# A gate's loads and heads' results in rings of tiles, attention steps counted by time, in a hybrid attention and retention layer

## The chip, the core and the metric

The kernel runs on one core of a Trainium2 chip. The metric is the device time of one execution, in microseconds. The core has a matrix engine (TensorE, PE in the rows; the load of its weights is PEld), VectorE (DVE), ScalarE (ACT), GpSimd (POOL) and SyncE (SP), which here issues most DMAs. Each engine takes its instructions in a fixed order. A chip-wide memory (DRAM) holds inputs, weights and spilled partial results; SBUF holds the tiles, PSUM the banks in which matmuls add up.

## The reference

One layer over 256 latent tokens and 256 context tokens of width 4096: a modulated RMS norm, one input projection of 14336 columns, differential attention in eight heads A (two softmax maps a head) and two-way retention in eight heads B, a SiLU gate on each, one output projection, and a residual with a gate. Cut to what matters:

```python
mod = silu(c) @ ada_w + ada_b
shift, scale, gate = split(mod, 3)
h = rms_norm(x, norm_w) * (1 + scale) + shift          # hc likewise from ctx, c_ctx
proj = h @ w_in                                        # dq dk dv dg rq rk rv rg
pc = hc @ w_ctx                                        # c_dk c_dv c_rk c_rv
o_d = diff_attention(dq, k_all, v_all, lam)            # 8 heads A, 256 wide
o_d = rms_norm(o_d, subln_w) * (1 - lam_init) * silu(dg)
o_r = rms_norm(retention(rq, rk, rv), ret_norm_w) * silu(rg)   # 8 heads B
y = concatenate([o_d, o_r]) @ w_out
return x + gate * y
```

## The kernel before

All products are float32 made of three passes: weights and activations are split into a high and a low part (whi, wlo and h), and each block of 128 rows of depth is hi x hi, hi x lo, lo x hi (L405 to L407). The depth of 4096 is 32 blocks, "kt". A **unit** is two kt of one head's columns: its weights are loaded by SP into a raw tile (three buffers, L387), ScalarE casts them to whi (L392), VectorE subtracts for wlo (L393), three buffers each, and PE multiplies them with 4 row tiles (K and V of latent and context tokens) or 2 (Q and gate of latent tokens). So a head has K/V units on four PSUM banks and Q/G units on two; the pool `mm` has six banks. A head of A is 512 columns wide, of B 384.

The normed input h arrives late, because its modulation needs a product with ada_w. So the work is staged. First, K/V of all A heads for the first ten kt while the modulation is made; then `first_parts`: for each head as many kt as are there, with partial sums copied to a kvqg tile and stored to DRAM (`store_part`, L523, ACT's queue), while VectorE makes the rest of the modulation (L322). Then `rests`: for A0 to A7 and B0 to B7 the remaining units, 104 of A (16, 16, 14, 12, 12, 12, 12, 10) and 140 of B (four heads with 19, four with 16). Four units before the end of a half the partial sums are loaded back (`load_part`, L518, SP's queue) into a kvqg tile, and after the last unit VectorE adds the banks to it (L500), which frees the banks. Last, the output projection, L1061, whose products are called psO.

In `rests`, three things run beside the products. *Attention*: when a head's units are over, `attend` puts its generator (`attA` or `attB`) into the list `tasks`; `bg_step` takes one step of the first in the list. attA has 16 steps, attB 12. Heads are taken strictly one after the other; a step touches PE, ScalarE, VectorE and GpSimd in turn. attA begins with norms (L748), ends its use of K and V with the split of V's second half (L723) and of Q/G with the output's transposes. `to_B` drains the list, closes the pool of attA's tiles and opens attB's. *The gate*: `gate_task` multiplies the last third of ada_w with c on VectorE, 128 loads of 512 KB (L938) and 128 steps (L952); at the end of each quarter the sum is split into gah and gal, which take a buffer each of the tags whi and wlo, until PE has summed them (pg, L963). *Weight loads* of the next unit.

The function `between`, called after each unit, takes one attention step, two when more than one head waits, and gate steps at 132 over the number of units less 8.

The pool `a4` has 39 slots (SLOTS) of 4 KB a partition: h takes one for each kt (22 once the first ten kt are used up), and kvqg tiles, gate loads, their sums and the B heads' outputs take theirs as they come free. What runs in which order on an engine is settled when the program is built, by a scheduler that takes the order of the program as priority; a load is issued when a slot is free for it.

Of the kernel before, what the change touches and what calls it, by code (L numbers as in the profile page):

```python
# [10 lines left out]
F32 = mybir.dt.float32  # L11
# [7 lines left out]
P = 128  # L19
D = 4096  # L20
KT = D // P
# [22 lines left out]
T_COL = 0.457e-3  # L44
# [33 lines left out]
def hybrid_kernel(es, tc, x, c, ctx, c_ctx, norm_w, ada_w, ada_b, w_in, q_norm_w, k_norm_w,  # L78
# [12 lines left out]
    a4 = es.enter_context(tc.tile_pool(name="a4", bufs=SLOTS, side="right"))  # L91
# [13 lines left out]
    def aux_tile(shape, name):  # L105
        return aux.tile(shape, F32, name=name, tag="aux")
# [243 lines left out]
    for half in range(2):  # L350
        ss = adap.tile([P, 2, NX], F32, name=f"ss{half}", tag="ss")
        for i in range(NX):
# [4 lines left out]
            for q in range(2):  # L357
                g = 2 * i + q
# [81 lines left out]
    def run_units(units):  # L440

        it = iter(units)
        nxt = next(it, None)
        if nxt is not None:
            nxt[0].prepare()
        while nxt is not None:
            (u, post), nxt = nxt, next(it, None)
            if nxt is not None:
                nxt[0].prepare()
            u.run()  # L450
            post()
# [13 lines left out]
    def evict(dst, src):  # L465
        evict_flip[0] ^= 1
        if evict_flip[0]:
            nc.scalar.copy(dst, src)
        else:
            nc.vector.tensor_copy(dst, src)  # L470

    class Head:

        def __init__(self, kind, h):
# [5 lines left out]
        def dst(self, rt, qg):  # L480
            i = 2 if qg else rt // 2
            if self.t[i] is None:
                self.t[i] = a4.tile([P, 2, self.ncol], F32, name=f"kvqg{self.name}_{i}", tag="a4")
            return self.t[i][:, rt % 2, :]

    def head_units(hd, qg, ktseq, part=False, rest=False, tag=""):
# [39 lines left out]
    def pairs(a, b):  # L526
        r = []
        while a < b:
            n = min(2, b - a)
            r.append((a, n))  # L530
            a += n
        return r
# [83 lines left out]
    kdone = {(nm, qg): K1 if nm[0] == "A" and not qg else 0 for nm in heads for qg in range(2)}  # L616

    def first_parts():

        items = [(f"B{h}", 0) for h in range(HB)] + [(f"A{h}", 1) for h in range(HA)] + [(f"B{h}", 1) for h in range(HB)]  # L620
        for nm, qg in items + [(f"A{h}", 0) for h in range(HA)]:
            hd = heads[nm]
            a, b = kdone[nm, qg], ada2.avail
            if a < b and not (a > 0 and ada2.done):
                kdone[nm, qg] = b
                nrt = 2 if qg else 4
                spare = FILL * 2 * 3 * nrt * hd.ncol * T_COL - (0.2 + 2 * hd.ncol * 1.05e-3)
                for u in head_units(hd, qg, pairs(a, b), part=True, rest=a > 0, tag=f"p{a}"):
                    yield u, lambda spare=spare: ada2.spend(spare)

    run_units(first_parts())
    while not ada2.done:
        ada2.spend(1.0)
# [86 lines left out]
    def split(hi, lo, src):  # L720

        nc.scalar.copy(hi, src)  # L722
        nc.vector.tensor_tensor(lo, src, hi.bitcast(F32), op=ALU.subtract)  # L723
# [207 lines left out]
    GW = 1024  # L931
    GATE_STEPS = D // GW * (KT + 1)

    def gate_task():
        def load(v):
            cb, kt = divmod(v, KT)
            raw = a4.tile([P, GW], F32, name=f"graw{cb}_{kt}", tag="a4")
            nc.sync.dma_start(raw, ada_w[kt * P:(kt + 1) * P, 2 * D + cb * GW:2 * D + (cb + 1) * GW])  # L938
            return raw

        n = D // GW * KT
        ahead = [load(0), load(1)]
        for v in range(n):
            cb, kt = divmod(v, KT)
            raw = ahead.pop(0)
            if v + 2 < n:
                ahead.append(load(v + 2))
            if kt == 0:
                acc = a4.tile([P, GW], F32, name=f"gacc{cb}", tag="a4")
                nc.vector.tensor_scalar(acc, raw, cT[:, 0, kt:kt + 1], None, op0=ALU.mult)  # L950
            else:
                nc.vector.scalar_tensor_tensor(acc, raw, cT[:, 0, kt:kt + 1], acc, op0=ALU.mult, op1=ALU.add)  # L952
            yield
            if kt == KT - 1:
                ah = wpool.tile([P, GW], F32R, name=f"gah{cb}", tag="whi", bufs=3)
                al = wpool.tile([P, GW], F32R, name=f"gal{cb}", tag="wlo", bufs=3)
                split(ah, al, acc)
                gb = a4.tile([P, GW], F32, name=f"gb{cb}", tag="a4")
                nc.scalar.dma_start(gb[0:1], ada_b[0:1, 2 * D + cb * GW:2 * D + (cb + 1) * GW])
                for q in range(GW // 512):  # L960
                    pg = aux_tile([P, 512], f"pg{cb}_{q}")
                    for i, a in enumerate((ah, al)):
                        nc.tensor.matmul(pg[0:32], onesr, a[:, q * 512:(q + 1) * 512], start=i == 0, stop=i == 1)  # L963
                    nc.vector.tensor_tensor(gb[0:1, q * 512:(q + 1) * 512], pg[0:1, :], gb[0:1, q * 512:(q + 1) * 512], op=ALU.add)
                nc.scalar.dma_start(g_dram[0:1, cb * GW:(cb + 1) * GW], gb[0:1])
                yield


    tasks = []

    def bg_step():
        while tasks:
            try:
                next(tasks[0])
                return
            except StopIteration:
                tasks.pop(0)

    def bg_drain():
        while tasks:  # L980
            bg_step()

    gate = gate_task()
    atB = [None]

    gate_due = [0.0, sum(len(pairs(a, KT)) for a in kdone.values()) - 8]

    def between():
        bg_step()
        if len(tasks) > 1:  # L990
            bg_step()
        gate_due[0] += GATE_STEPS / gate_due[1]
        while gate_due[0] >= 1:
            gate_due[0] -= 1
            next(gate, None)

    def to_B():
        between()
        bg_drain()
        atA_cm.__exit__(None, None, None)  # L1000
        atB_cm = tc.tile_pool(name="attB", bufs=1, side="left")
        atB[:] = [atB_cm.__enter__(), atB_cm]

    def rests():
        for nm in [f"A{h}" for h in range(HA)] + [f"B{h}" for h in range(HB)]:
            hd = heads[nm]
            us = []
            for qg in range(2):
                a = kdone[nm, qg]
                if a < KT:  # L1010
                    us.append(head_units(hd, qg, pairs(a, KT), rest=a > 0))
                else:
                    load_part(hd, qg)

            def attend(hd=hd):
                tasks.append(attA(hd) if hd.kind == "A" else attB(hd, atB[0]))
                between()

            flat = [(u, between) for q in us for u in q]
            if nm == "B0":  # L1020
                k = min(4, len(flat) - 2)
                flat[k] = (flat[k][0], to_B)
            flat[-1] = (flat[-1][0], attend)
            yield from flat

    run_units(rests())
    while next(gate, 0) is None:
# [33 lines left out]
    for nb in range(NB):  # L1061
        bank = Bank(f"psO{nb}", 2)
        start, end = out_ends(nb, bank)
        for i, s in enumerate(order):
            xs = (lambda k, r, s=s: o_t[s][:, 0, k, r * P:(r + 1) * P],
                  lambda k, r, s=s: o_t[s][:, 1, k, r * P:(r + 1) * P])
# [42 lines left out]
```

## Time and profile before

| | us |
|---|---|
| median of three executions | 2659.67 (2658.77 to 2660.13) |
| the profiled execution | 2661.34 |
| its span, first to last instruction | 2659.6 |
| PE busy | 2515.6 |
| VectorE busy | 1820.5 |
| ScalarE busy | 887.6 |
| mean granted clock of PE | 0.969 of full |

Busy times are unions of an engine's instructions over the span. The ends of matmuls are modelled, so a busy PE is not a PE at its peak. Times in rows are in microseconds from the span's start. A wait is put down to the instruction that came last by the semaphores. Products of an A head in `rests` write psA, of a B head psB.

### The profile page before, as it was taken

How to read it: one execution, taken by the hardware profiler on the slowest of the kernel's cores; microseconds unless marked ns; L12 is line 12 of the kernel's file. 1: busy time of each engine (PE TensorE's matmuls, PEld its weight loads, DVE VectorE, ACT ScalarE, POOL GpSimd, SP SyncE). 2: the span in 40 equal slices, each digit the busy share in tenths (PEclk: the TensorE clock that was granted, in tenths of full speed). 3: DMA queues.
4: the chain of work that ended last, by engine and by line, in shares of the span. 5: the costliest groups of instructions: out<-in, count | busy, mean ns of one | idle time of the engine just before them, and what ended most of it. 6: DMA issues, size and time to landing. Idle time of an engine off the chain costs nothing. (4 is left out here: it accounts for less than half of the span.)

```text
span 2659.6 us, 33974 instructions
## 1 busy us (share of the span) xinstructions
PE 2515.6 (95%) x12354; PEld 2140.1 (80%) x12354; DVE 1820.5 (68%) x2438; ACT 887.6 (33%) x1384; POOL 42.7 (2%) x47
## 2 busy tenths in 40 slices
PE   7999999999998999997899999997488999999999
PEld 4677799987988888876688788997388999778887
DVE  4756939799589489797866777564577666644444
ACT  4211222343443122222333344433233333433333
POOL 0000000000000000000000000000000000000000
PEclk8999999999999999997899999999699999999999
DMA  9977858889789678677866566442256564666765
GB/s 319 293 249 223 283 180 269 265 277 328 236 256 314 230 266 258 222 239 260 308 207 191 186 210 190 152 142 74 99 164 226 194 196 153 218 196 209 223 211 171
DMA packets 471417, 590.82 MB, mean 222 GB/s; under 512 B 32521, under 2 KB 353353, under 8 KB 471249
## 3 DMA queue, kind: packets, MB, share of 16 engines
q1 hardware_dynamic: 453392, 544.40, 64.0%
q10 hardware_dynamic: 17856, 44.25, 4.6%
q8 instruction: 97, 1.59, 0.3%
q14 instruction: 72, 0.58, 0.1%
HBM read 551.81 MB, written 36.72 MB: 221 GB/s over the span
## 5 line engine op out<-in xcount | busy, mean ns | idle before, releaser
L322 DVE SCALAR_TENSOR_TENSOR acc<-ada,cT,acc 128x1024 f32<-128x1024 f32 (+1 forms) x372 | 427.9, 1190 | 0.0
L406 PE MATMUL psB<-wloB,h 128*128 128x384 f32 x896 | 305.2, 341 | 2.4 <-DVE wloB L393 2.4
L407 PE MATMUL psB<-whiB,h 128*128 128x384 f32 x896 | 303.3, 339 | 0.0
L405 PE MATMUL psB<-whiB,h 128*128 128x384 f32 x896 | 285.1, 340 | 5.7 <-DVE kvqgB L500 5.7
L393 DVE TENSOR_TENSOR wloO<-rawO,whiO 128x1024 fp32r<-128x1024 f32 x128 | 156.8, 1225 | 173.8 <-ACT whiO L392 173.6
L406 PE MATMUL psA<-wloA,h 128*128 128x512 f32 x560 | 229.4, 410 | 12.0 <-DVE wloA L393 11.9
L405 PE MATMUL psA<-whiA,h 128*128 128x512 f32 x560 | 212.8, 405 | 17.6 <-ACT whiA L392 17.6
L407 PE MATMUL psA<-whiA,h 128*128 128x512 f32 x560 | 226.0, 406 | 0.0
L392 ACT CAST whiO<-rawO 128x1024 fp32r<-128x1024 f32 x128 | 134.5, 1052 | 214.8 <-PE psO L407 172.3
L406 PE MATMUL psO<-wloO,o 128*128 128x512 f32 x512 | 204.1, 399 | 0.3 <-DVE wloO L393 0.3
L407 PE MATMUL psO<-whiO,o 128*128 128x512 f32 x512 | 203.4, 398 | 0.0
L393 DVE TENSOR_TENSOR wloB<-rawB,whiB 128x768 fp32r<-128x768 f32 x140 | 133.2, 955 | 85.0 <-ACT whiB L392 84.4
L392 ACT CAST whiB<-rawB 128x768 fp32r<-128x768 f32 x140 | 116.2, 834 | 216.1 <-PE psB L407 138.5
L405 PE MATMUL psO<-whiO,o 128*128 128x512 f32 x512 | 184.3, 399 | 1.2 <-ACT o L722 1.2
L952 DVE SCALAR_TENSOR_TENSOR gacc<-graw,cT,gacc 128x1024 f32<-128x1024 f32 x124 | 158.8, 1281 | 38.7 <-DMA graw<-in_ada_w_dram 37.6
L392 ACT CAST whiA<-rawA 128x1024 fp32r<-128x1024 f32 x104 | 109.0, 1050 | 201.4 <-PE psA L407 135.4
L405 PEld LDWEIGHTS psB<-whiB,h 128*128 128x128 f32 x896 | 167.7, 190 | 7.5 <-DVE kvqgB L500 6.1
L406 PEld LDWEIGHTS psB<-wloB,h 128*128 128x128 f32 x896 | 169.3, 189 | 4.9 <-DVE wloB L393 4.0
L407 PEld LDWEIGHTS psB<-whiB,h 128*128 128x128 f32 x896 | 169.4, 189 | 0.5
L393 DVE TENSOR_TENSOR wloA<-rawA,whiA 128x1024 fp32r<-128x1024 f32 x104 | 126.5, 1221 | 49.3 <-ACT whiA L392 48.7
L405 PEld LDWEIGHTS psA<-whiA,h 128*128 128x128 f32 x560 | 106.7, 193 | 45.3 <-ACT whiA L392 20.9
L406 PEld LDWEIGHTS psA<-wloA,h 128*128 128x128 f32 x560 | 108.7, 194 | 42.1 <-DVE wloA L393 17.0
(495 smaller groups left out, 5178.9 us busy)
## 6 DMA issues: line engine op xcount, KB each, us to landing
ada<-in_ada_w_dram SPq DMA_DIRECT2D x512, 256.0 KB, 4.6
graw<-in_ada_w_dram SPq DMA_DIRECT2D x128, 512.0 KB, 7.4
rawO<-in_w_out_dram SPq DMA_DIRECT2D x128, 512.0 KB, 4.6
rawA<-in_w_in_dram SPq DMA_DIRECT2D x208, 256.0 KB, 3.7
rawB<-in_w_in_dram SPq DMA_DIRECT2D x140, 256.0 KB, 3.0
p_dramA<-kvqgA ACTq DMA_DIRECT2D x40, 512.0 KB, 4.3
kvqgA<-p_dramA SPq DMA_DIRECT2D x40, 512.0 KB, 6.3
rawB<-in_w_in_dram SPq DMA_DIRECT2D x140, 128.0 KB, 2.4
```

What stands on the lines that cost most here:

```text
L322: nc.vector.scalar_tensor_tensor(acc[v], w, cv, acc[v], op0=ALU.mult, op1=ALU.add)
L392: nc.scalar.copy(hi, raw)
L393: nc.vector.tensor_tensor(lo, raw, hi.bitcast(F32), op=ALU.subtract)
L405: nc.tensor.matmul(pt[:, :ncol], a, hi, start=f, stop=False)
L406: nc.tensor.matmul(pt[:, :ncol], a, lo, start=False, stop=False)
L407: nc.tensor.matmul(pt[:, :ncol], b, hi, start=False, stop=e)
L952: nc.vector.scalar_tensor_tensor(acc, raw, cT[:, 0, kt:kt + 1], acc, op0=ALU.mult, op1=ALU.add)
```

## The change

Before the first parts a ring of four tiles of a4 is made, before the rests one of nine; `Head.dst` takes the next tile of the ring instead of a new slot, so a head's three tiles are three places of it, and a tile is free for its next user when its last reader is through. The gate's loads take three fixed tiles in turn. `between` gets the unit and adds its time on PE (kt x 3 x row tiles x columns x T_COL) to an account, from which a step of attention is taken for each 2.8 us, or 2.0 us when two or more heads wait. The gate is spread over the units less 40 instead of less 8. `to_B` runs at the end of B0's units instead of after its fifth, and a head's attention joins the list after the steps of its last unit instead of before them.

```diff
--- before.py
+++ after.py
@@ -469,6 +469,12 @@
         else:
             nc.vector.tensor_copy(dst, src)
 
+
+    ring, turn = [], [0]
+
+    def new_ring(name, n):
+        ring[:] = [a4.tile([P, 1024], F32, name=f"{name}{i}", tag="a4") for i in range(n)]
+
     class Head:
 
         def __init__(self, kind, h):
@@ -480,7 +486,11 @@
         def dst(self, rt, qg):
             i = 2 if qg else rt // 2
             if self.t[i] is None:
-                self.t[i] = a4.tile([P, 2, self.ncol], F32, name=f"kvqg{self.name}_{i}", tag="a4")
+                if ring:
+                    turn[0] = (turn[0] + 1) % len(ring)
+                    self.t[i] = ring[turn[0]][:, 0:2 * self.ncol].rearrange("p (r n) -> p r n", r=2)
+                else:
+                    self.t[i] = a4.tile([P, 2, self.ncol], F32, name=f"kvqg{self.name}_{i}", tag="a4")
             return self.t[i][:, rt % 2, :]
 
     def head_units(hd, qg, ktseq, part=False, rest=False, tag=""):
@@ -628,6 +638,7 @@
                 for u in head_units(hd, qg, pairs(a, b), part=True, rest=a > 0, tag=f"p{a}"):
                     yield u, lambda spare=spare: ada2.spend(spare)
 
+    new_ring("ring", 4)
     run_units(first_parts())
     while not ada2.done:
         ada2.spend(1.0)
@@ -934,11 +945,12 @@
     def gate_task():
         def load(v):
             cb, kt = divmod(v, KT)
-            raw = a4.tile([P, GW], F32, name=f"graw{cb}_{kt}", tag="a4")
+            raw = graw[v % 3]
             nc.sync.dma_start(raw, ada_w[kt * P:(kt + 1) * P, 2 * D + cb * GW:2 * D + (cb + 1) * GW])
             return raw
 
         n = D // GW * KT
+        graw = [a4.tile([P, GW], F32, name=f"graw{i}", tag="a4") for i in range(3)]
         ahead = [load(0), load(1)]
         for v in range(n):
             cb, kt = divmod(v, KT)
@@ -981,13 +993,18 @@
             bg_step()
 
     gate = gate_task()
+    new_ring("ring", 9)
     atB = [None]
 
-    gate_due = [0.0, sum(len(pairs(a, KT)) for a in kdone.values()) - 8]
-
-    def between():
-        bg_step()
-        if len(tasks) > 1:
+    gate_due = [0.0, sum(len(pairs(a, KT)) for a in kdone.values()) - 40]
+
+    bg_due = [0.0]
+
+    def between(u):
+
+        bg_due[0] += u.nk * 3 * u.nrt * sum(g[1] for g in u.segs) * T_COL / (2.8 if len(tasks) < 2 else 2.0)
+        while bg_due[0] >= 1:
+            bg_due[0] -= 1
             bg_step()
         gate_due[0] += GATE_STEPS / gate_due[1]
         while gate_due[0] >= 1:
@@ -995,7 +1012,6 @@
             next(gate, None)
 
     def to_B():
-        between()
         bg_drain()
         atA_cm.__exit__(None, None, None)
         atB_cm = tc.tile_pool(name="attB", bufs=1, side="left")
@@ -1008,20 +1024,19 @@
             for qg in range(2):
                 a = kdone[nm, qg]
                 if a < KT:
-                    us.append(head_units(hd, qg, pairs(a, KT), rest=a > 0))
+                    us += head_units(hd, qg, pairs(a, KT), rest=a > 0)
                 else:
                     load_part(hd, qg)
 
-            def attend(hd=hd):
+            def attend(u, hd=hd):
+                between(u)
+                if hd.name == "B0":
+                    to_B()
                 tasks.append(attA(hd) if hd.kind == "A" else attB(hd, atB[0]))
-                between()
-
-            flat = [(u, between) for q in us for u in q]
-            if nm == "B0":
-                k = min(4, len(flat) - 2)
-                flat[k] = (flat[k][0], to_B)
-            flat[-1] = (flat[-1][0], attend)
-            yield from flat
+
+            for u in us[:-1]:
+                yield u, lambda u=u: between(u)
+            yield us[-1], lambda u=us[-1], attend=attend: attend(u)
 
     run_units(rests())
     while next(gate, 0) is None:
```

## Rows read from the trace of the kernel before

**Rows 1.** The page, section 2: tenths of 40 slices of 66.5 us; PE busy, granted clock.

```profile
PE   7999999999998999997899999997488999999999
...
PEclk8999999999999999997899999999699999999999
```

**Rows 2.** Busy time by stretch: length, each engine's us (instructions), PEclk, DMA share, GB/s.

```profile
1232.00:1300.00 68.00, 47.88 (x169) 35.10 (x168) 56.37 (x70) 15.80 (x37) 2.50 (x1) 0.80 1.04 382
1300.00:1650.00 350.00, 346.44 (x1571) 280.75 (x1570) 242.83 (x365) 142.55 (x270) 13.92 (x12) 1.00 0.64 201
1650.00:1841.00 191.00, 190.18 (x1115) 187.03 (x1114) 117.09 (x220) 72.88 (x154) 8.15 (x7) 1.00 0.44 132
1841.00:1935.00 94.00, 39.05 (x150) 27.56 (x148) 50.49 (x120) 28.76 (x77) 5.82 (x7) 0.63 0.25 89
1935.00:2050.00 115.00, 107.16 (x611) 103.59 (x612) 92.20 (x142) 39.56 (x65) 2.16 (x4) 0.96 0.60 202
```

**Rows 3.** The same view, instructions on psB alone: PE, PEld and DVE.

```profile
1650.00:1841.00 191.00, 176.87 (x968) 167.32 (x966) 5.09 (x10) 1.00 0.44 132
1841.00:1935.00 94.00, 0.12 (x1) 0.12 (x1) 0.73 (x2) 0.63 0.25 89
```

**Rows 4.** Timeline of SP, 1727 to 1915: start, us, line, transfer, count (issues merged).

```profile
1728.10 3.71 SPq L518 DMA_DIRECT2D kvqgB<-p_dramB  x2
...
1741.11 162.61 SPq L387 DMA_DIRECT2D rawB<-in_w_in_dram  x56
...
1905.58 0.68 SPq L518 DMA_DIRECT2D kvqgB<-p_dramB  x1
```

**Rows 5.** Timeline of DVE: attention starts (L748), A heads' additions (L500), last V split.

```profile
1558.22 0.17 DVE L748 TENSOR_SCALAR rsA<-ssA 128x12 f32<-128x12 f32 x1
...
1560.63 1.28 DVE L500 TENSOR_TENSOR kvqgA<-psA,kvqgA 128x512 f32<-128x512 f32 x2
...
1612.15 1.28 DVE L500 TENSOR_TENSOR kvqgA<-psA,kvqgA 128x512 f32<-128x512 f32 x2
...
1647.92 0.16 DVE L748 TENSOR_SCALAR rsA<-ssA 128x12 f32<-128x12 f32 x1
...
1723.37 0.17 DVE L748 TENSOR_SCALAR rsA<-ssA 128x12 f32<-128x12 f32 x1
...
1797.66 0.16 DVE L748 TENSOR_SCALAR rsA<-ssA 128x12 f32<-128x12 f32 x1
...
1889.06 0.69 DVE L723 TENSOR_TENSOR vvA<-kvqgA,vvA 128x512 fp32r<-128x512 f32 x1 [3.25 <-ACT vvA L722]
```

**Rows 6.** First instruction of each A and B head's attention: ns min/median/max, first and last start.

```profile
L748 DVE TENSOR_SCALAR rsA<-ssA x8: 164/170/175, 1264.7 to 1859.5; 128x12 f32<-128x12 f32 x8
...
L862 DVE TENSOR_SCALAR nlbB<-lg x8: 146/147/147, 1902.7 to 2138.7; 128x1 f32<-128x1 f32 x8
```

**Rows 7.** Weight loads (rawA), issue to landing: first 1228 to 1292, then 1300 to 1650.

```profile
DMA to landing us min/median/max: 7.3/8.1/9.3
...
DMA to landing us min/median/max: 2.7/3.4/4.8
```

**Rows 8.** Waits of ACT, 1232 to 1300: us in total, times, longest.

```profile
ACT whiA L392 <- DMA rawA<-in_w_in_dram: 22.5, 6, 6.0
```

**Rows 9.** Waits of DVE, 1300 to 1850.

```profile
DVE gacc L952 <- DMA graw<-in_ada_w_dram: 26.7, 21, 2.6
```

**Rows 10.** Busy time by stretch, instructions on gacc alone: DVE, ACT.

```profile
1935.00:2282.00 347.00, 67.02 (x53) 2.08 (x2) 0.99 0.57 187
```

**Rows 11.** Busy time by stretch, all engines as in rows 2: late in the first parts.

```profile
800.00:850.00 50.00, 44.55 (x239) 41.21 (x240) 49.32 (x47) 17.28 (x23) 0.00 (x0) 1.00 0.98 314
```

**Rows 12.** Waits of SP's queue, 1820 to 1940.

```profile
SPq L387 <- DVE nlbB L862: 59.0, 1, 59.0
```

**Rows 13.** Timelines of ACT and PE: the gate's pair is made, and read.

```profile
1707.36 1.05 ACT L722 CAST gah<-gacc 128x1024 fp32r<-128x1024 f32 x1 [1.19 <-PE psB L407]
...
1898.08 0.64 PE L963 MATMUL pg<-gah,onesr 128*32 128x512 f32 x1 [1.79 <-DVE jk2A L828]
```

## The prediction

> **What bounds the kernel now.** I read the page first: the two rows by slices. PE is busy in nine tenths or more of nearly every slice, so time can only come from the slices in which PE or PEclk falls: 18 and 19, and 27 to 30, counted from 0 [rows 1]. Then I read the table of busy time by stretch, to price them [rows 2]. From 1300 to 1650 (products of the A heads) 1571 matmuls take 350 us, 0.22 us each; from 1650 to 1841 (products of the B heads) 1115 take 191 us, 0.171 us each. At these paces 1232 to 1300 holds 169 x 0.22 = 37 us of work and loses **31**; 1841 to 1935 holds 150 x 0.171 = 26 us and loses **68**; 1935 to 2050 holds 611 x 0.171 = 104.5 us and loses **10.5**.
>
> What ends last in the large hole? Of products there is one in 1841 to 1935, against 968 in the stretch before [rows 3]: PE does nothing there but attention, at a granted clock of 0.63 [rows 2]. The next product waits until a head's PSUM banks are emptied (L500). That addition needs a kvqg tile whose load SP issues at 1905.58; the kvqg loads before it went out at 1728.10, and from 1741 on SP issues 56 weight loads and no load for a kvqg tile or for the gate [rows 4]. That reads as a pool without a free slot for either: at 1841 the heads hold 11 slots of a4 (A6 three, A7 three, B0 three, B1 two), beside 22 tiles of h.
>
> Why are so many heads in flight? Attention is one serial chain. A3's begins at 1558.2 and A4's at 1647.9: **90 us** for a head beside products of A. The products of A5 end at 1560.6 and those of A6 at 1612.2: **52 us** for a head [rows 5]. So attention falls behind, from 1264.7 for A0 to 1859.5 for A7 [rows 6]. A7's takes from 1859.5 to 1902.7, where B0's begins: **43 us**, with PE to itself [rows 6]. The second split of a head's V, the last read of its K/V tiles, stands at 1889.1 for A7, 69% of the way [rows 5].
>
> The loss at 1232 to 1300 has another cause. DMA is at 1.04 of its engines and 382 GB/s [rows 2]; a weight load lands after 8.1 us, against 3.4 us in 1300 to 1650 [rows 7]; the cast of the weights waits for it 22.5 us, in six waits [rows 8]. The gate's loads, 512 KB each, take whatever slots are free there.
>
> **The change part by part.** The profiled execution took 2661.34 us, 1.7 over its span and 1.7 over the median of 2659.67. I add up against 2661.3 and take off 1.7 at the end.
>
> *Gate ring of three.* The same 128 loads and 128 steps; none is added. At most three gate loads stand before a weight load. Landing of weights in 1232 to 1300 then lies between 3.4 and 8.1 us [rows 7]; I take the middle, since up to nine kvqg loads can still go out there, so half of the 22.5 us: **-11** (0 to -22). Later, a gate load has been under way for two steps when its turn comes. From 1300 to 1850 VectorE stood 26.7 us in 21 waits for a gate load [rows 9], in the queue in which the attention's steps stand too; over the six heads of that stretch this is 4 us a head off the 90. The other side: the gate is no longer throttled by slots. 53 of its steps run after 1935, at 67.0/53 = 1.26 us [rows 10]; moved into 1300 to 1650 they would raise VectorE from 242.8 to 310 of 350 us. That is priced under the rivals.
>
> *Head ring of nine in the last stage.* Three heads hold tiles: K/V of head n+3 can't be loaded before head n's attention has split its V the second time. Against 11 slots this is tighter. PE runs past a missing tile as far as its six banks go (K/V of a head take four, Q/G two). With attention at 90 us, tiles are short first at A6: A3's come free at 1558 + 0.69 x 90 = 1620, and its banks are full at 1612 [rows 5]; with the load's landing PE waits some 18 us. For A7 put it per head: in 52 us of products attention does 52/90 = 58% of a head; the rest takes 42% of 43 us = 18 us with PE idle. In the B products a head is longer (360 of the 968 products in 191 us: 71 us [rows 3]) and attention shorter (A5's starts at 1723.4, A6's at 1797.7: 74 us [rows 5]); 71/74 leaves 4% of 43 = 2 us a head, for B0 to B2 6. **Stops: 18 + 18 + 6 = 42 us instead of 78.5**; less 8 for the 4 us a head that the gate's waits free (five heads, 0.42 of each); plus 4 for clock lost behind the two stops of 18 us (1935 to 2050 has 0.96 of the clock behind a long one [rows 2]: 4% of 100 us). The two ends: all 78.5 come back if attention keeps up, and the stops grow to 80 if it slows.
>
> *Ring of four in the parts before.* A head stores one or two tiles, with eight units (16 us) or more of products to each. Of the slices 8 to 17, nine show PE at nine tenths or more and one at eight [rows 1]. I take 0; the cover is that a tile's store has landed before its turn comes again, and if it has not, ACT waits on p_dram and PE for banks: 5 us either way.
>
> *Steps paid by time.* A K/V unit of an A head (2 x 3 x 4 x 512 columns at T_COL, 0.457 ns, = 5.6 us) buys 2.0 steps, a Q/G unit 1.0, of B 1.5 and 0.75; with two heads waiting 1.4 times as many. Before, each bought one, or two. A head has 10 to 16 units of A and 16 steps. In the program A7's steps end with B0's fifth unit; in the rows they run from 1859.5 [rows 6], two heads of products later. A chain that trails its place by so much is not held back by it: 0, at best 10 us for A0.
>
> *to_B at the end of B0, gate over 204 units instead of 236.* The drain at B0's fifth unit did not hold B0's products, which ran at full pace to 1841 [rows 3]. 0, but it hangs on A7's attention being over by the end of B0 in the order of the engines; where it is not, B0's attention waits for it as it does now. The earlier gate returns five slots before the B heads' o tiles need them; that is in the 10.5 already counted.
>
> **Sum.** 2661.3 - 78.5 + 42 - 8 + 4 - 11 = 2609.8; less 1.7: **2608**.
>
> **The rivals.** *Attention keeps up.* If its interval beside A products falls to about 65 us, nine tiles suffice and no stop is left: 2661.3 - 78.5 - 11 - 1.7 = 2570; with all 22 at the front 2559. For it: VectorE's waits for gate loads go. Against it: PE takes its instructions in order, and at each change of engine the chain stands behind products.
>
> *The ring is what PE waits for* (slower). More gate work per us stands beside attention and the splits of weights. Where VectorE was busy 49.32 of 50 us, PE was busy 44.55 [rows 11]. If the chain goes from 90 to 107 us a head, A5 already stops PE (5 us), A6 and A7 25 each, B0 to B2 8 each: 79 us, as much as now, and 5% of the 350 us for late splits, 17: 2661.3 - 78.5 + 79 + 4 + 17 - 11 - 1.7 = 2670. It decides from an interval of about 105 us. The Trainium skill (Perfetto Trace Analysis, Optimization Strategy) says that bubbles that repeat on the engine that should be saturated can mean too few buffers for the next tile; by it nine tiles instead of eleven would give a bubble a head, which is this rival. The trace shows one hole, at eleven, and so can't say more.
>
> *It does not do what it says.* SP stood 59.0 us in one wait, at a weight load [rows 12], and the kvqg load is behind it. The gate's pair gah, gal holds one of three whi buffers from 1707.4 until pg reads it at 1898.1 [rows 13], and the change leaves the pair in that pool. If that wait makes the hole, and not the slots, the hole moves and stays: 2661.3 - 11 + 5 - 1.7 = 2654. Against it: between 1741 and 1834 SP passed dozens of weight loads and still issued no kvqg load [rows 4].
>
> **How the numbers follow.** Forecast 2608 (2595 to 2645): 0.44. Attention keeps up (2540 to 2595): 0.24. No effect on the hole (2645 to 2665): 0.12. Ring too small (2665 to 2710): 0.20. A measurement of this kernel can tell about 0.2%, 5 us, from no change: 2654 to 2665 is the same. The first two cases and a third of the third are faster: 0.72; the rest of the third is the same: 0.08; slower 0.20. The range is 2548 to 2682: it leaves out the far ends of the two outer cases, together some 0.2.
>
> **What would show it.** Right: no stretch of over 40 us without a product between 1650 and 2000; stops of 15 to 20 us at A6 and A7, ended by L500 or by a load of L518 that waited for a V split (L723) of three heads earlier; attention starts 80 to 90 us apart beside A products; weight loads landing in 4 to 6 us after the gate begins; the gate over by about 1800. Wrong: starts 65 us apart or less (faster) or 105 and more (slower); VectorE over 45 of 50 us from 1300 to 1650; a new hole where pg waits. What would make the forecast fail above all is another interval of the attention than the rows of before give.

## The result, and the profile after

The changed kernel takes 2622.3 us (median, 2620.1 to 2624.3) against 2659.9 of the kernel before on the same chip: a ratio of 0.986 (95% interval 0.984 to 0.987), 37.6 us faster. The forecast was 2608 in a range of 2548 to 2682, with 0.72 on faster. The profiled execution has a span of 2618.3 us against 2659.6.

First the rows that answer to [rows 1]: tenths of 40 slices of 65.5 us, PE busy and granted clock.

```profile
PE   7999999999988999998899998799999999899999
...
PEclk8999999999999999998899999899999999999999
```

The hole of slices 27 to 30 is gone. In its place stand two slices with 8 and 7 (24 and 25), one more 8 in the first parts (11) and one where the projection begins (34). The same stretches as in [rows 2], same columns:

```profile
1232.00:1300.00 68.00, 55.31 (x220) 42.19 (x219) 52.04 (x68) 20.57 (x42) 2.50 (x1) 0.90 0.95 320
1300.00:1650.00 350.00, 327.07 (x1433) 260.63 (x1432) 273.04 (x387) 133.15 (x259) 14.03 (x11) 0.97 0.74 251
1650.00:1841.00 191.00, 180.75 (x1002) 169.58 (x1001) 114.62 (x229) 76.65 (x162) 10.98 (x9) 0.98 0.40 117
1841.00:1935.00 94.00, 94.00 (x558) 93.08 (x557) 54.23 (x110) 37.32 (x78) 3.66 (x3) 1.00 0.43 124
1935.00:2050.00 115.00, 112.61 (x683) 111.02 (x682) 83.50 (x136) 42.33 (x68) 2.85 (x4) 1.00 0.64 203
```

From 1841 to 1935 PE runs 558 matmuls in place of 150, and from 1232 to 1300 220 in place of 169. But from 1300 to 1650 it runs 138 fewer: that is where part of the gain went back.

Stretches of the clock compare badly once two kernels have drifted apart. So the products from the first parts on were numbered in both traces, 0 to 9791: A's rests begin at 3888, B's at 5568, the projection at 8256. The table gives, between two numbers, the time, PE's other matmuls (nearly all attention) and the us that PE stood idle.

```
products        before: us  other  idle   after: us  other  idle   difference
   0 to 3900       841.4                     849.3                    +7.9
3900 to 4350       159.6     56   29.1       143.8     50   17.9     -15.8
4350 to 5250       237.5    160    3.0       235.2    126    4.3      -2.3
5250 to 5700       108.7     72    0.6       166.0    160   28.6     +57.3
5700 to 6450       148.8    120    0.8       149.6    130    0.3      +0.8
6450 to 6600       125.3    165   55.8        31.9     38    0.0     -93.4
6600 to 7200       130.3    119    7.0       118.8    121    0.0     -11.5
7200 to 8400       240.1    185    0.4       250.1    237    3.7     +10.0
8400 to 8550        47.0     19    5.9        52.3     34    8.5      +5.3
8550 to 9790       290.5      0    0.0       290.5      0    0.0       0.0
```

Five things happened: the first parts lost 8 us, the start of the rests gained 16, the last A heads lost 57, the hole gave 105, and the end lost 15.

*Where the 57 come from.* Starts of the attention of A0 to A4 (timeline of VectorE in the kernel after, as in [rows 5]):

```profile
1269.76 0.17 DVE L759 TENSOR_SCALAR rsA<-ssA 128x12 f32<-128x12 f32 x1
...
1397.64 0.17 DVE L759 TENSOR_SCALAR rsA<-ssA 128x12 f32<-128x12 f32 x1
...
1507.87 0.17 DVE L759 TENSOR_SCALAR rsA<-ssA 128x12 f32<-128x12 f32 x1 [0.55 <-ACT jkA L757]
...
1587.64 0.17 DVE L759 TENSOR_SCALAR rsA<-ssA 128x12 f32<-128x12 f32 x1
...
1649.95 0.17 DVE L759 TENSOR_SCALAR rsA<-ssA 128x12 f32<-128x12 f32 x1 [0.36 <-ACT jkA L757]
```

A0 takes 128 us and A1 110, against 99 and 102 before; then 80 and 62. The ring hands the lateness on. The loads of A5's and A6's K/V (timeline of SP, first fence; the second of A6's is inside the merged row) go out within 1 us of the splits of A2's and A3's V (timeline of VectorE, second):

```profile
1541.77 0.34 SPq L528 DMA_DIRECT2D ring<-p_dramA  x1
...
1565.69 0.34 SPq L528 DMA_DIRECT2D ring<-p_dramA  x1
...
1617.55 27.43 SPq L528 DMA_DIRECT2D ring<-p_dramA  x3
```

```profile
1541.02 0.68 DVE L734 TENSOR_TENSOR vvA<-ring,vvA 128x512 fp32r<-128x512 f32 x1
...
1564.97 0.69 DVE L734 TENSOR_TENSOR vvA<-ring,vvA 128x512 fp32r<-128x512 f32 x1 [5.67 <-ACT vvA L733]
...
1616.80 0.68 DVE L734 TENSOR_TENSOR vvA<-ring,vvA 128x512 fp32r<-128x512 f32 x1
```

SP's queue stood 40 us in such waits (its waits from 1540 to 1720: us, times, longest):

```profile
SPq L528 <- DVE vvA L734: 40.2, 6, 15.5
```

The other end of that chain, in the waits of VectorE and of PE from 1540 to 1720: the addition (now L510) waits for the load, the next product waits for the addition.

```profile
DVE ring L510 <- DMA ring<-p_dramA: 13.2, 9, 3.9
...
PE psA L405 <- DVE ring L510: 12.5, 5, 4.4
PE psB L405 <- DVE ring L510: 5.6, 2, 3.6
```

Of the 57 us, 28 are idle time of PE. In the rest PE runs 88 more other matmuls, and all of them at a mean granted clock of 0.92 in place of 1.00.

*The gate.* Its steps by stage (busy time of VectorE on the gate's line; number in brackets):

```profile
1300.00:1400.00 100.00, 43.51 (x34) 1.00 0.95 330
1400.00:1500.00 100.00, 44.16 (x35) 1.00 0.93 323
...
1600.00:2000.00 400.00, 0.00 (x0) 0.98 0.41 121
2000.00:2100.00 100.00, 39.58 (x31) 1.00 0.80 267
```

It runs at full rate beside A0 and A1, which see 84 of its first 96 steps. Step 96 stands at 1515 (not by 1500, as the expectations below have it), the next at 2003, and the last at 2085, not by 1800.

### The profile page after: what moved, and what is told of

It reads as the page before. It is cut to its first block, busy times and chain, and to the rows that moved or that the text cites. A ratio compares the mean times of both kernels' runs of the same rounds, so it can differ in the third digit from the quotient of the medians.

```text
span 2618.3 us, 34049 instructions
## 1 busy us (share of the span) xinstructions
PE 2508.7 (96%) x12354; PEld 2134.8 (82%) x12354; DVE 1813.7 (69%) x2438; ACT 885.9 (34%) x1384; POOL 47.9 (2%) x47
## 5 line engine op out<-in xcount | busy, mean ns | idle before, releaser
L322 DVE SCALAR_TENSOR_TENSOR acc<-ada,cT,acc 128x1024 f32<-128x1024 f32 (+1 forms) x372 | 428.3, 1189 | 0.0
L407 PE MATMUL psB<-whiB,h 128*128 128x384 f32 x896 | 303.3, 339 | 0.0
L405 PE MATMUL psB<-whiB,h 128*128 128x384 f32 x896 | 277.1, 339 | 8.1 <-DVE ring L510 5.6
L964 DVE SCALAR_TENSOR_TENSOR gacc<-graw,cT,gacc 128x1024 f32<-128x1024 f32 x124 | 158.4, 1278 | 18.7 <-DMA graw<-in_ada_w_dram 18.3
L406 PEld LDWEIGHTS psA<-wloA,h 128*128 128x128 f32 x560 | 110.4, 197 | 36.3 <-DVE wloA L393 10.5
```

Of the source, the lines that this page charges most:

```text
L322: nc.vector.scalar_tensor_tensor(acc[v], w, cv, acc[v], op0=ALU.mult, op1=ALU.add)
L405: nc.tensor.matmul(pt[:, :ncol], a, hi, start=f, stop=False)
L406: nc.tensor.matmul(pt[:, :ncol], a, lo, start=False, stop=False)
L407: nc.tensor.matmul(pt[:, :ncol], b, hi, start=False, stop=e)
```

## Experiments

Each ran beside the kernel before; ratios are to that. "Stop" below is the time from product 5250 to 5700, 108.7 us in the kernel before and 166.0 in the changed one.

**What the gate's work does to the attention.** Most of the gate was left out, so this is a test and no version to use:

```diff
+    KG = 1
-            cb, kt = divmod(v, KT)
+            cb, kt = divmod(v, KG)
```

> The changed kernel, but the gate reads one block of 128 rows of each quarter instead of 32: 4 loads and 4 steps instead of 128 each; the other 124 are left out, the sums by PE stay in their places. It takes 158 us of VectorE's time and 65 MB of loads away. Theory 1 (the gate's work on VectorE slows the attention of A0 and A1, and the ring hands that on as stops): A0 and A1 take at most 100 us each, A3 starts at 1555 or earlier, the stops shrink to 30 us or less, the 1232 to 1300 stretch gives up to 8 more: 2588 us (2575 to 2600). Theory 2 (the attention is slow for PE's sake, whatever VectorE does): starts of A0 to A3 within 10 us of 1270, 1398, 1508, 1588 and 2612 to 2622.

2559.1 us, 0.962 (0.961 to 0.964). The starts of A0 to A3:

```profile
1263.64 0.17 DVE L759 TENSOR_SCALAR rsA<-ssA 128x12 f32<-128x12 f32 x1
...
1343.34 0.17 DVE L759 TENSOR_SCALAR rsA<-ssA 128x12 f32<-128x12 f32 x1 [3.86 <-ACT jkA L757]
...
1419.02 0.16 DVE L759 TENSOR_SCALAR rsA<-ssA 128x12 f32<-128x12 f32 x1
...
1501.58 0.17 DVE L759 TENSOR_SCALAR rsA<-ssA 128x12 f32<-128x12 f32 x1 [4.20 <-ACT jkA L757]
```

A0 takes 80 us in place of 128, and the stop 115.7 in place of 166.0, with the same nine tiles and the same PE work. Busy time from 1300 to 1500 (columns as above), here and then in the changed kernel:

```profile
1300.00:1500.00 200.00, 200.00 (x924) 162.74 (x923) 122.40 (x204) 86.52 (x172) 8.51 (x8) 1.00 0.48 150
```

```profile
1300.00:1500.00 200.00, 197.61 (x888) 159.69 (x887) 182.27 (x223) 72.21 (x114) 6.71 (x5) 1.00 0.94 327
```

In the second row PE is hardly less busy; VectorE goes from 122 to 182 of 200 us, and the chain that passes through it again and again takes 1.6 times as long. Theory 1 holds, and is worth more than it said: 63 us, not 34.

The run takes the gate's steps and its loads away together. Which of them the chain feels can be estimated from the two traces by following A0's attention back by tile names. Its instructions on VectorE start in sum some 38 us behind their last input in the changed kernel and 9 us here, those on PE some 54 and 46. So most of the 48 us is waiting ahead of VectorE's instructions.

VectorE's busy share does not give the size, though. In the run with the head rings alone (below) A0 takes 97 us, with 39 gate steps beside it and VectorE busier than in the changed kernel:

```profile
1273.00:1370.00 97.00, 92.52 (x408) 74.16 (x409) 93.42 (x123) 35.55 (x69) 3.61 (x3) 0.96 1.01 362
```

By the same estimate its waits before VectorE are 30 us and those before PE 39. In the run with twelve tiles (below) A0 takes 128 us with VectorE at 0.78. Over all runs A0 and A1 took 76 to 82 us without gate steps beside them and 93 to 128 with. How much slower they get, the order of the engines' instructions may set as well; that was not tried apart.

A slower gate was tried first:

```diff
-            raw = graw[v % 3]
+            raw = graw[v % 1]
-        ahead = [load(0), load(1)]
+        ahead = [load(0)]
```

> The changed kernel, but the gate has one tile in turn instead of three, so a gate load can only go out when the step before it has been taken. In the changed kernel 96 of the gate's 128 steps stand between 1231 and 1500 us, VectorE is busy 43 to 47 of 50 us there, and the attention of A0 and A1 takes 128 and 110 us instead of 99 and 102 before the change. Theory 1 (the attention's chain is slowed by gate work on VectorE, and the stops at A5 to A7 are this lateness handed on by the ring of nine): with a step each 6 to 7 us, A0 and A1 take about 100 us each, A3's attention starts at some 1560 instead of 1588, and the stops shrink by as much: 2597 us (2588 to 2608). Theory 2 (the ring of nine alone sets the stops, whatever the gate does): starts of A0 to A3 move, the time stays at 2622 (2617 to 2628). Theory 3 (the gate's pair that holds one of three buffers of whi from 1419 to 1555 and from 1666 to 1822 makes the stops): the pair's hold moves with the gate, the stops move with it, and no wait for a V split ends them; time 2615 to 2635.

2713.0 us, 1.019 (1.018 to 1.021): no theory's number. A0 takes 102 us as theory 1 said, but the steps, 9 in 50 us, now go on to 1775, and A1 to A3 take 110, 101 and 89; the stop is 173.6. The same work spread out slows more heads less. And a new stretch of 70 us without a product stands at 2127 to 2197; the last experiments come back to it.

**The account of steps.**

```diff
-        bg_due[0] += ... / (2.8 if len(tasks) < 2 else 2.0)
-        while bg_due[0] >= 1:
-            bg_due[0] -= 1
-            bg_step()
+        bg_step()
+        if len(tasks) > 1:
+            bg_step()
```

> The changed kernel with the old account of attention steps: one after each unit, two when more than one head waits; the rings, the gate's pace and the pools' change stay as in the changed kernel. From the first start of an attention (A0) to the fourth (A3) the changed kernel takes 318 us, the kernel before 294, the run with the head rings alone 281; the stops beside A5 to A7 cost 58 us in the changed kernel and 31 in the run with the head rings alone. Theory 1 (steps by time slow the first heads: they put more of a chain on PE, ScalarE and VectorE that these can't take yet): 281 to 295 us from A0 to A3, stops of about 30, time 2595 us (2585 to 2605). Theory 2 (the prediction's: the account of steps is worth nothing): 2622 (2616 to 2628), A0 to A3 in 310 to 325.

2619.2 us, 0.985 (0.984 to 0.986); from the start of A0 to that of A3 it takes 314 us, the stop 165.5. Theory 2: no difference.

**The rings alone, and the gate's ring alone**, each put into the kernel before:

> The kernel before with one part of the change: rings of four and nine for the heads' tiles; the gate takes free slots as before, its pace, the attention steps and the place of the pools' change are those of before. Theory 1 (the ring of nine takes the hole away, and the start of the rests stays as it was): 8 us lost in the first parts, nothing gained from 1232 to 1300, stops beside A5 to A7 that come from loads waiting for a V split, no stretch over 40 us without products: 2637 us (2625 to 2650). Theory 2 (the hole was made by something else, as the order of steps or the pools' change in B0's fifth unit): a hole of over 60 us stays after 1800 and the time is 2655 to 2690.

2647.9 us, 0.995 (0.994 to 0.997). Products 6450 to 6600 take 32.0 us: the old hole is gone without any other part, so it was the slots. The stop is 140.4. But products stand still once more from 1962 to 2021, where SP issues gate loads and no weight load. Theory 1, with one stop of over 40 us that it ruled out.

> The kernel before with one part of the change: the gate's loads take three fixed tiles. Theory 1: the stretch 1232 to 1300 gives back 11 to 15 us, the hole that the heads' slots make at 1841 stays, and since the gate now runs at full rate beside A0 and A1 the attention is some 25 us later and the hole that much longer: 2672 us (2660 to 2680). Theory 2 (gate work does not slow the attention): only the gain of the start: 2646 (2640 to 2650).

2648.9 us, 0.996 (0.994 to 0.997). The number is theory 2's, the mechanism neither's. From 3900 to 4350 the rests gain 12.9 us, as forecast; by product 5700 they are 18 ahead. A0 and A1 take 105 and 118 us. At 6600 the products are 4 ahead: the lead goes in a stop of 13.5 us at 1777.6, just ahead of the hole. The hole then begins at 1841.1, behind the same product as before, and no product runs until 1931.7, behind the start of B0's attention at 1903.4 (1902.7 before). Behind it the lead is back (18 us at 7200, 10.5 at 8400). So little of what is gained ahead of the hole is left at its end, which another chain sets; what brings the rest back was not traced.

**The ring of four taken out of the changed kernel.**

```diff
-    new_ring("ring", 4)
     run_units(first_parts())
```

> The changed kernel without the ring of four: in the first parts each head takes a slot of the pool as before; the ring of nine and all else stay. By the number of products done, the changed kernel falls 14 us behind the kernel before between 700 and 860 us, and still is 8 us behind when the rests begin. Theory 1 (the ring of four does it): the first parts run as before the change, the rests begin 8 us earlier: 2614 us (2610 to 2618). Theory 2 (it is the order that the scheduler happens to find, with no link to the ring): the first parts keep a loss of about that size: 2622 (2618 to 2626).

2610.4 us, 0.981 (0.980 to 0.983): theory 1; product 3900, just behind the start of the rests, stands at 1164.2 and not 1174.5 (1166.3 before). Time of VectorE in the sums of the modulation (L322) from 700 to 750: the changed kernel, then this one:

```profile
700.00:750.00 50.00, 22.36 (x18) 1.00 0.84 264
```

```profile
700.00:750.00 50.00, 0.00 (x0) 1.00 0.71 208
```

With the ring of four the modulation's next sums (L320, tiles of the same pool) start some 50 us earlier (712.8 in place of 759.7), beside the splits of B's weights. That reads as slots which the heads now leave free; the slots themselves were not traced. All engines of the changed kernel in that stretch (VectorE is the third pair):

```profile
700.00:750.00 50.00, 45.52 (x253) 43.10 (x251) 47.51 (x58) 22.73 (x35) 0.00 (x0) 1.00 0.84 264
```

VectorE is busy 47.5 of 50 us and PE runs 253 matmuls where without the ring of four it runs 292. The run with the head rings alone, which has this ring too, starts the sums at 712.2 and is as late at product 3900 (1175.2).

**More tiles.**

```diff
-    new_ring("ring", 9)
+    new_ring("ring", 12)
-            raw = graw[v % 3]
+            raw = graw[v % 2]
```

With two tiles the gate also loads one step ahead instead of two.

> The changed kernel with a ring of twelve tiles instead of nine in the last stage; to have room the gate has two tiles in turn instead of three. Theory 1 (the loads that wait for a V split of three heads earlier make the stops): with four heads' room the loads of A5 to A7 no longer wait so long, the stops of 58 us beside A5 to A7 fall to 10 to 25, part comes back later as attention that is then late in B: 2597 us (2585 to 2612). Theory 2 (PE's own order of products and attention steps makes the stops, the tiles are only what is seen last): the stops stay, 2618 to 2632.

2649.1 us, 0.996 (0.995 to 0.998), above both theories; the profiled execution, at 2660.5, is the longest of the eight. The stop falls to 130.0, as theory 1 said, and SP waits for V splits from 1540 to 1720 as little as this:

```profile
SPq L528 <- DVE vvA L734: 10.6, 5, 8.1
```

But the gate's last quarter comes at 2045 to 2131, and no product runs from 2067 to 2134. The Trainium skill (Perfetto Trace Analysis, Optimization Strategy) says that a gap that repeats on the engine that should be saturated can mean that there are too few buffers for the next tile. In this place the runs agree: three more tiles, with one fewer for the gate, took 36 us off the stop. The run without the gate's work took 50 off it with no tile more.

**The gate's pair out of whi and wlo.**

```diff
-                ah = wpool.tile([P, GW], F32R, name=f"gah{cb}", tag="whi", bufs=3)
+                ah = a4.tile([P, GW], F32R, name=f"gah{cb}", tag="a4")
```

> The changed kernel, but the gate's pair gah and gal takes slots of the pool a4 instead of a buffer each of whi and wlo. In the changed kernel the pair stands from 1419 to 1555, 1666 to 1822, 1886 to 2009 and 2086 to 2159, and the products have two of three buffers then. Theory 1 (the chain of the attention sets the stops): no change of theirs, at most the 13 us for which PE waits for casts of A's weights shrink a little: 2620 us (2612 to 2626). Theory 2 (the third rival of the prediction in a smaller size: two buffers instead of three stop PE): the stops at 1550 to 1700 lose half or more: 2595 (2585 to 2608).

2638.0 us (2626.7 to 2638.5), 0.991 (0.989 to 0.992), so neither: the stop is 174.0, unmoved, which speaks for theory 1, and the time is worse than its range, with 17 us more from 7200 to 8400. The profiled execution is the shortest of the five (2626.7), so some 11 us of the median are not in these rows.

**The gate's work put elsewhere**, in the kernel without the ring of four. A quarter's tiles are first written from a late head's tile, so that its loads can't run ahead (lines of the second of three runs; the quarters' steps are also spread over other numbers of units):

```diff
+        if dep is not None:
+            for t in graw:
+                nc.vector.tensor_scalar(t[:, 0:1], dep.t[2][:, 0, 0:1], 0.0, None, op0=ALU.mult)
...
+                if hd.name == "B1":
+                    gate[0] = gate_task([0, 1], hd)
...
+    gate[0] = gate_task([2, 3], heads["B7"])
```

> The kernel of the run without the ring of four (2610 us), with the gate's whole work kept but placed anew: the first quarter at the start of the rests, the second and third only after B1's products (their three tiles are first written from B1's Q/G tile, so no load can go earlier), the fourth beside the output projection. With all four quarters' work gone the run with one block a quarter took 2559 us, A0 to A3 80, 76 and 83 us apart, and stops of 7 us instead of 57. Theory 1 (gate work on VectorE beside A's attention is what makes the stops): A0 some 100 us, A1 and A2 about 80, stops of 15 to 25 us beside A5 to A7, a few us each beside B and the projection: 2578 us (2565 to 2592). Theory 2 (the gate's loads, when they come in a block in SP's queue ahead of weight loads, stop the products wherever they stand, as in the run with the slow gate): a stop of 40 us or more in the B products, 2605 to 2650.

> As the run before it, but no quarter at the start of the rests: the first two after B1's products, the other two beside the output projection, where VectorE is busy 24 of 50 us and DMA at 0.70. Theory 1: A0 to A3 as without the gate's work (80 us apart), stops of 10 us or less, and the start 1232 to 1300 gains up to 8 us more; 128 us of VectorE's time and 32 MB of loads beside the projection cost little while DMA stays under 1.0: 2568 us (2555 to 2585). Theory 2 (the loads of the projection's weights come late when 32 MB stand beside them): the projection takes 10 to 30 us longer than 373: 2580 to 2600.

> As the run with one, two and one quarters, but the fourth also in the B products, none beside the projection. Theory 1: A's stops as there (15 to 25 us); the 96 steps in B take VectorE from some 30 to 40 or more of 50 us, B's attention, with 36 to 60 us a head against products of 60, has room for part of it: 2585 us (2570 to 2605). Theory 2 (VectorE's work costs the same beside B as beside A): the stops move into B, 2605 to 2625.

2628.3, 2619.0 and 2648.9 us; ratios 0.988 (0.987 to 0.990), 0.984 (0.982 to 0.986) and 0.996 (0.994 to 0.997). All three miss theory 1's times. (Two quarters take 64 steps of 1.26 us, 81 us of VectorE's time and not the 128 of the second text.) The first lies in the range of its theory 2, with the stop that this named; the other two lie above both of theirs. In A theory 1 holds for the starts: with one quarter in front A0 takes 103 us, with none 78. The stop is 141.2 with one quarter, 32 us over the kernel before where 15 to 25 were expected, and 114.9 with none, as expected; by product 7050 the second run is 127 us ahead of the kernel before. Then each loses the lead: no product runs from 1957 to 2011, 1926 to 1986 and 1926 to 2003. SP's queue of the second of them:

```profile
1912.99 4.44 SPq L387 DMA_DIRECT2D rawB<-in_w_in_dram  x3
1918.82 13.90 SPq L950 DMA_DIRECT2D graw<-in_ada_w_dram  x8
1933.60 0.33 SPq L528 DMA_DIRECT2D ring<-p_dramB  x1
1934.79 6.49 SPq L950 DMA_DIRECT2D graw<-in_ada_w_dram  x4
...
1977.93 6.77 SPq L950 DMA_DIRECT2D graw<-in_ada_w_dram  x4
1988.52 1.92 SPq L387 DMA_DIRECT2D rawB<-in_w_in_dram  x4
```

From 1918.8 to 1988.5 these are 32 gate loads, spaced by steps of VectorE, and no weight load. In ScalarE's timeline the split of that quarter stands just ahead of the first weight load:

```profile
1984.38 1.05 ACT L732 CAST gah<-gacc 128x1024 fp32r<-128x1024 f32 x1 [3.33 <-DVE gacc L969]
```

In all six kernels with such a stop the weights come back 3 to 5 us after gah is written:

```
                        gah      next weight load
slow gate              2194.8    2198.0
head rings alone       2019.0    2023.9
ring of twelve         2132.4    2135.7
quarters 1, 2, 1       2009.0    2012.9
quarters 0, 2, 2       1984.4    1988.5
quarters 1, 3, 0       2001.4    2005.0
```

The changed kernel has it in small: no weight load goes out from 2077.2 to 2089.9, and gah is written at 2086.4.

So in the last run the end of a quarter (split, sum on PE) was moved to a later unit of the program, behind the time at which the steps are through. The steps beside B also go from 0.825 to 1 a unit:

```diff
             if kt == KT - 1:
-                ah = wpool.tile([P, GW], F32R, name=f"gah{cb}", tag="whi", bufs=3)
+                accs[cb] = acc
...
+            if nun[0] == at_:
+                gate_end(cb)
```

> As the run with no quarter at the start, two beside B and two beside the projection, but the end of a quarter (its split into gah and gal, which take a buffer of whi and wlo, and the sum on PE) stands later in the program: 70 and 96 units after B1 instead of some 40 and 80, and 52 and 86 units into the projection. The loads and steps themselves are the same. That run was 127 us ahead of the kernel before at product 7050 and then lost 60 in one stop, in which SP issued 32 gate loads and no weight load; in it and in four other runs the weight loads came back 3 to 5 us after gah was written. Theory 1 (units that stand after gah in the program can't get their whi buffer before gah has its own, and so the products wait until the quarter's steps are through): with the end behind the steps no such stop is left; some 8 us lost to VectorE beside B and 10 beside the projection: 2555 us (2545 to 2575). Theory 2 (the gate's loads and steps cost this wherever they stand in B): a stop of 40 us or more stays, 2595 to 2625.

2587.7 us (2584.9 to 2593.8), 0.973 (0.972 to 0.975). The B products (psB) from 1925 to 2000, in the run with quarters 0, 2 and 2 and then here:

```profile
1925.00:2000.00 75.00, 14.26 (x62) 13.25 (x61) 0.00 (x0) 0.61 0.76 254
```

```profile
1925.00:2000.00 75.00, 68.28 (x370) 64.92 (x370) 2.97 (x6) 0.98 0.93 317
```

The stop is gone, with the same 32 loads and steps in nearly the same place (1920 to 1999, 1918 to 1983 in the other run). So the place of the quarter's end made it, as far as the small change of pace leaves that open. That the reason is the order in which tiles of whi are given out fits all six rows and was not tried apart from ScalarE's own order, in which gah stands ahead of the next weight cast. The time is 33 us over what was expected, and in neither theory's range. From 7200 to 8400 this kernel takes 280.3 us where the changed one takes 250.1: PE is idle 17.7 us in place of 3.7 and runs 32 more other matmuls, beside 51 gate steps in place of 25. That the steps cost this was not tried apart. The projection takes 9 us longer.

## Why the prediction was right or wrong

The time lies in the range. The sum promised 10 us too much in the profiled spans (-51.5 forecast, -41.3 measured), and the median lies 14 us over the forecast. By its own steps:

*Gate ring at the start, -11:* measured -15.8 from 3900 to 4350, and -12.9 with this part alone. Right. Weight loads land after 5.2 us there (8.1 in [rows 7]), the cast waits 10.9 us in four waits (22.5 in [rows 8]).

*The hole is a pool without slots:* right; the heads' rings alone removed it, with the gate's pair left in whi and wlo, and the gate's ring alone did not. Rival three falls as it was put: the hole did not stay. But the pair that it named is where six other kernels stopped for 53 to 77 us.

*Stops of 42 in place of 78.5, less 8, plus 4:* from 4350 to 7200 this forecasts -40.5; measured -49.1. The mechanism is the one forecast, loads that wait for a V split of three heads earlier; it begins at A5, not A6, PE's idle time from 5250 to 5700 is 28.6 us, and the longest time without a product there is 11.3 us, where stops of 15 to 20 were named as the sign. The size is right only because two errors met. The chain was taken at 80 to 90 us a head; it was 128 and 110 at the front. Once products stand still it is 62 to 73, so both of the prediction's signs of a wrong interval came up in one trace. The hole also gave more than 78.5 by products, since 165 of PE's other matmuls stood in it. They did not vanish: 88 more stand in the stop, 52 more after 7200.

*"Less 8": gate waits freed.* This step failed. VectorE's waits for gate loads do shrink, from 37.6 to 18.3 us over the kernel, but the gate that no longer waits takes VectorE itself. The second rival had this mechanism (more gate work beside attention) and gave it 0.20; it came true at the front, at 128 us a head, over the 105 from which it was to decide. That it did not make the kernel slower fits that it struck two heads and not all: after step 96, at 1515, the gate stood until 2003. Without any gate work A0 takes 80 us, so about 20 of the 99 before were the gate's too; [rows 9] shows the waits and not that.

*Ring of four, 0 (up to 5):* failed: +7.9, and 11.9 us between the medians with it and without. The prediction looked at the ring's own cover, the stores; the cost came from another user of the pool, which got its slot earlier.

*Steps by time, 0:* right. *to_B:* not tried apart; the hole went with the old place as well as with the new one. *Gate over 204 units, in the 10.5:* the gate is over at 2085 and not by 1800. How dear a late quarter can be (53 to 77 us) shows in six runs; which part of the change keeps it cheap here was not tried apart.

*The end, +15:* not in the sum. The row of L862 in [rows 6] can't place the later B heads, since that instruction runs up to two heads ahead; the first write of dlB, which each head's attention needs, can. At product 7200 (2019.9) the changed kernel is in B2's attention, which starts at 1992.0, and B3's starts at 2052.9. Before, product 7200 (2076.5) finds B3's near its end: B4's starts at 2081.6. Attention that was done in the hole is now done beside the last B products. A stall that is also the time in which a late chain catches up can't be taken out whole.

## What to carry to other kernels

A pool that is full is also a brake: before a change frees slots, list who else waits for one, and ask which engine that user will take and which chain passes through it. A serial chain can feel an engine long before that engine bounds the kernel: here A0 and A1 took 76 to 82 us with VectorE at 57% to 61%, and 93 to 128 with it at 68% to 96%. A ring behind the chain turns its lateness into stops. So look at the interval of the chain; the busy share warns, but did not give the size. In an order fixed when the program is built, a rare big job that takes a tile of a common ring should have its place in the program behind the time when its inputs are ready: that move took away a stop of 60 us and 31 us of the time. The best version here, at 0.973, is the changed kernel without the ring of four and with the gate moved so.

## What the runs showed of the hardware

A high rate of loads cost the products little here: from 1300 to 1500 the DMA share was 0.94 at 327 GB/s, weight loads landed after 4.7 us (median of 1300 to 1650) against 3.4 before, and PE was busy 197.6 of 200 us with 888 matmuls (924 without the gate's loads, at 0.48).

The granted clock fell with stops that left PE busy most of the time. From 1540 to 1700 PE was busy 130 of 160 us, its longest time without a product was 11.3 us, and the clock was 0.90:

```profile
1540.00:1700.00 160.00, 129.77 (x544) 101.07 (x543) 89.07 (x172) 57.96 (x129) 7.86 (x7) 0.90 0.35 109
```

Of the two levels, 2.4 and 1.2 GHz, the lower shows in single products: from 1540 to 1720 the median of the first pass of an A product is 397 ns and the longest 796. The prediction allowed 4 us for clock behind two stops; a clock of 0.90 over 160 us is some 16 (an estimate), and here it came with many short stops, as it did before with one long one (0.63 in [rows 2]).
